# Two blocks instead of one pass mixing and routing first, in plain fp32, and the second of them is gathered for one expert table and dense for the other

## The chip, the cores and the metric

The kernel runs on one core of a Trainium2 chip. The metric is device time in microseconds of one execution: 1673.88 us is the median of three runs of the kernel before (1673.73 to 1687.47). TensorE does the matrix products, VectorE (DVE) and ScalarE (ACT) the elementwise work, GpSimd (POOL) issues the gathers of table rows, and SyncE (SP) issues nearly all other transfers.

## The reference, cut to what matters

512 tokens of width 1024 are worked in four blocks of 128. One layer is mixing, then a product-key expert lookup (PEER), then a last norm:

```
xn = rmsnorm(h);  z = xn @ w_in + b_in              # 1024 -> 3840, split into q k v pool gates
y_a = sliding_window_attention(q, k, v) @ w_attn_up # window 128: own block and the one before
y_p = multiscale_pool(pz) @ w_pool_up
h   = h + (sigmoid(ga) * y_a + sigmoid(gp) * y_p) @ w_o
xn  = rmsnorm(h);  q = xn @ w_query                 # 8 heads, two halves of 128
sc  = q . sub_keys -> top 16 per half -> 256 sums -> top 16 = idx, softmax = g
a   = gelu(u_tab[idx] . xn)                         # 128 experts for each token, of 16384
h   = h + sum(g * a * v_tab[idx]);  out = rmsnorm(h)
```

The two expert tables have 16384 rows of 1024 floats, 64 MB each. For a token block the lookup can be done in two ways. It can be **gathered**: 128 times, one row per token is fetched (128 rows, 512 KB) and multiplied on DVE. Or it can be **dense**: the whole table is streamed through TensorE for all tokens of the block, and the gate matrix (zero for the experts not chosen) picks the results.

## The kernel before, in words

Weights come as tiles of 128x1024 (512 KB). A matrix product is made in one of two ways. Plain fp32 uses the tile as it lands. The three-term form (`mm3`, L114) splits both operands into a high and a low part of the faster fp32r kind and adds hi*hi, hi*lo and lo*hi; each streamed tile then costs a cast on ACT (`wh`, L127) and a subtraction on DVE (`wl`, L121).

The program has these stages. `lead` (L203) takes block 0 alone through mixing and key scores in plain fp32, 128 columns wide. `mixing`, `residual` and `scores` (L334, L580, L622) take blocks 1 to 3 through the same steps in the three-term form, 384 columns wide; beside it `tick` lets background work go on, which is the choice of block 0's experts (`select`) and its gathers (`gather`, L898: 128 rows of the first table, dotted on DVE at L906, and 128 of the second, added at L910). Then 128 expert tiles of the first table are streamed (`u_part`, L781): 24 matmuls of 384 columns each give all three blocks' products. Beside it, blocks 2 and 3 are chosen, and their gate matrices are built and written out (`onehot`, L729: for each 8 tokens eight Abs and eight Relu instructions on ACT, one comparison on DVE, eight plain matmuls, one copy on ACT). Block 1's products are stored (`late`), since its own 128 are later picked from them by element gathers.

In the last stage (`dense`, L856) 128 tiles of the second table are streamed for blocks 2 and 3: 12 matmuls of 512 columns per tile, the left sides made from the kept products (`ga`) and the gates (`gt`) by `mix`. Beside it `gather_late` (L877) fetches 128 rows of the second table for block 1 and adds them on DVE (L895). `final` writes the blocks.

The order of work is written out by hand: `Background` runs a generator until a credit is spent, and `R_A`, `T_Z`, `T_A` and the like are the credits per step. In the last stage each engine's program order is the written order. Rows fetched by POOL wait in a ring of `ROWS` buffers, streamed tiles in a ring of `RAW`.

Of the kernel before, what the change touches and what calls it, by code (L numbers as in the profile page):

```python
# [11 lines left out]
F32 = mybir.dt.float32  # L12
# [7 lines left out]
P = 128  # L20
# [8 lines left out]
PH = 8  # L29
# [11 lines left out]
LB = 1  # L41
VB = 2
NV = 2
TU = SEQ - P
NT = TU // P
# [3 lines left out]
AJ = 4  # L49
# [12 lines left out]


class Layer:
    def __init__(self, ctx, tc, a):
# [6 lines left out]
        self.work, self.owed = [], 0.0  # L72
# [9 lines left out]
        self.natg = c.tile([P, D], F32, name="natg")  # L82
        self.svg = c.tile([P, 16, TOPK], F32, name="svg")
        self.sig = c.tile([P, 16, TOPK], U32, name="sig")
        self.eig = c.tile([P, P], I32, name="eig")
        self.gwg = c.tile([P, P], F32, name="gwg")
        self.hspill = nc.dram_tensor("hspill", (NBLK - 1, P, D), F32, kind="Internal").ap()
        self.ahead = nc.dram_tensor("ahead", (NKEY, P, TD), F32, kind="Internal").ap()
        self.late = nc.dram_tensor("late", (NKEY * P * P, 1), F32, kind="Internal").ap()
        self.spill = nc.dram_tensor("spill", (NG, P, NKEY, TG), F32, kind="Internal").ap()  # L90

    def consts(self):
# [6 lines left out]
        self.tok = self.c.tile([P, 1], I32, name="tok")  # L99
        self.nc.sync.dma_start(out=self.tok, in_=a["tok"])  # L100
# [22 lines left out]
    def weights(self, src, late=False):  # L123
        raw, hi, lo = (self.w.tile([P, D], t, name="w" + n, tag="w" + n, bufs=b)
                       for n, t, b in (("r", F32, RAW), ("h", F32R, WB), ("l", F32R, WB)))
        self.nc.sync.dma_start(out=raw, in_=src)
# [6 lines left out]
    def plan(self, keys):  # L133
        self.keys, self.ready = list(keys), []

    def fetch(self, name, i, look=LOOK):
        while self.keys and len(self.ready) <= look:
            n, j = self.keys.pop(0)
            self.ready.append(((n, j), self.weights(self.a[n][j])))
        key, w = self.ready.pop(0)  # L140
        assert key == (name, i)
        return w
# [11 lines left out]
    def transpose_split(self, x, n, hi, lo):  # L154
        nc = self.nc
        ps = self.big([P, n, P], "tr")
        for k in range(n):
            nc.tensor.transpose(ps[:, k, :], x[:, k * P:(k + 1) * P], self.ident)
        self.split(ps, hi, lo)

    def pair(self, pool, tag, nt=TU):
        return tuple(pool.tile([P, KD, nt], F32R, name=tag + n, tag=tag + n, bufs=1) for n in "hl")
# [18 lines left out]
    def z_block(self, f, xn, dst):  # L181
        w = self.fetch("w_in", f)
        ps = self.mm_tile(TU)
        for k in range(KD):
            if k == KD // 2:
                yield 1
            c = slice(k * P, (k + 1) * P)
            self.mm3(ps, (w[0][:, c], w[1][:, c]), (xn[0][:, k, :], xn[1][:, k, :]), k == 0, k == KD - 1)
        self.nc.scalar.activation(dst, ps, AF.Identity, bias=self.b_in[:, f:f + 1])

    def zq(self, mp, qs, xn, f):
        if f % 2 == 0:
            qs[f // 2] = mp.tile([P, 2, TU], F32, name="q", tag="q", bufs=3)
        return self.z_block(f, xn, qs[f // 2][:, f % 2, :])

    def tick(self, amount):
        for w in self.work:
            if not w.done:
                with self.tc.issue_after(self.lowered):
                    w.spend(amount)  # L200
                return

    def lead(self, mp, t2, t4, kT, vn, carry, g, prologue, rest, others):  # L203
        nc, a = self.nc, self.a
        one = self.m.tile([P, 3, KD, P], F32, name="mh", tag="mh", bufs=1)
        two = self.m.tile([P, 24, P], F32, name="ml", tag="ml", bufs=1)
        xT, att, mT = one[:, 0], one[:, 1], one[:, 2]
        gates, qa = two[:, :16], two[:, 16:]
        yT = mp.tile([P, 4, P], F32, name="yh", tag="yh", bufs=1)

        def raw(src):
            w = self.rows.tile([P, D], F32, name="row", tag="row")
            nc.sync.dma_start(out=w, in_=src)
            return w
# [12 lines left out]
        def across(src):  # L227
            ps = self.big([P, KD, P], "tr")
            for k in range(KD):
                nc.tensor.transpose(ps[:, k, :], src[:, k * P:(k + 1) * P], self.ident)  # L230
            nc.scalar.copy(xT, ps)

        def attended(c, po):
            nc.scalar.copy(att[:, c, :], po)

        def pooled(j, y):
            nc.vector.tensor_copy(yT[:, j, :], y)
# [40 lines left out]
        while active:  # L278
            step()
# [825 lines left out]
```

## Time and profile before

| what | value |
|---|---|
| median of 3 runs | 1673.88 us |
| the profiled execution | 1678.03 us |
| its span, first to last instruction | 1676.0 us |
| PE, DVE, ACT, POOL busy | 90%, 76%, 50%, 40% |
| granted TensorE clock, mean | 0.961 |
| moved by DMA | 476.41 MB, mean 284 GB/s |

A share of the whole span is a mean over stages that are limited by different things. So the rows below are cut by stage. PE is the matmuls, PEld the weight loads that overlap with them; a plain fp32 matmul appears as two instructions, so x16 is eight of them.

### The profile page before, as it was taken

Reading aid. Unit: us, or ns where it says so; the run is one execution under the profiler, and the core shown is the slowest. Engines: PE = TensorE matmul, PEld = TensorE weight load, DVE = VectorE, ACT = ScalarE, POOL = GpSimd, SP = SyncE. Lnnn points to the kernel's source line nnn. Section 1 sums busy time; section 2 is a strip of 40 time slices with the busy share of each in tenths; the row PEclk is TensorE's granted clock in tenths of the full one; section 3 lists DMA queues with packets and bytes.
Section 4 is the critical chain, followed back from the end, with each engine's and each line's share of the span. In section 5 each row is a group of like instructions: output and inputs, shape, how many; then the busy total and the mean of one; then the engine's idle time right before and its main releaser. Section 6 shows DMA issues by size and latency. Waiting matters only on the chain.

```text
span 1676.0 us, 23878 instructions
## 1 busy us (share of the span) xinstructions
PE 1515.9 (90%) x8234; PEld 1356.9 (81%) x8234; DVE 1276.3 (76%) x2395; ACT 835.7 (50%) x1663; POOL 668.8 (40%) x518
## 2 busy tenths in 40 slices
PE   6898979999779989789999999999789898888887
PEld 5797967899679979789999999999766665666665
DVE  2402878889857999977789876677379898898898
ACT  4411346643234333399994999833334343333344
POOL 0000010255520024544435544354277776676730
PEclk9998989999889999989999999999899999999999
DMA  7685242499973348789999999998689999999995
GB/s 270 229 296 206 70 162 94 161 349 341 363 263 105 129 157 295 258 289 344 334 356 316 381 354 345 360 323 313 188 278 357 357 343 369 358 376 372 347 358 206
DMA packets 189465, 476.41 MB, mean 284 GB/s; under 512 B 21408, under 2 KB 84896, under 8 KB 187040
## 3 DMA queue, kind: packets, MB, share of 16 engines
q1 hardware_dynamic: 128736, 270.31, 45.5%
q0 software_dynamic: 59392, 201.42, 34.1%
q10 hardware_dynamic: 1216, 3.15, 0.6%
q8 instruction: 65, 1.06, 0.3%
q14 instruction: 56, 0.46, 0.1%
HBM read 438.50 MB, written 35.78 MB: 283 GB/s over the span
## 4 chain that ended last, share of the span: by engine, by line
PE 28%; DMA 10%; ACT 9%; DVE 7%; issue 4%; POOL 1%; DVEq 0%; ACTq 0%; POOLq 0%
DMA wr<-v_experts 8%; PE mm L116 6%; PE mm L117 6%; PE mm L118 6%; DVE wl L121 4%; PE acc L117 4%; PE acc L118 3%; PE acc L116 3%; ACT wh L127 2%; ACT ohj L752 2%; ACT ohj L746 2%; PE pg L764 2%; ACT gs L765 1%; POOL act L882 1%; DVE h L895 1%
## 5 line engine op out<-in xcount | busy, mean ns | idle before, releaser
L121 DVE TENSOR_TENSOR wl<-wr,wh 128x1024 fp32r<-128x1024 f32 x315 | 385.5, 1225 | 199.0 <-ACT wh L127 196.7
L116 PE MATMUL mm<-xh,wh 128*128 128x384 f32 (+1 forms) x1408 | 486.3, 346 | 19.1 <-ACT gk L795 16.6
L127 ACT CAST wh<-wr 128x1024 fp32r<-128x1024 f32 x315 | 331.9, 1054 | 331.6 <-PE mm L117 239.0
L118 PE MATMUL mm<-xh,wl 128*128 128x384 f32 (+1 forms) x1408 | 479.7, 341 | 7.3 <-DVE wl L121 7.3
L117 PE MATMUL mm<-xl,wh 128*128 128x384 f32 (+1 forms) x1408 | 479.0, 340 | 5.6 <-DVE xl L121 5.6
L873 POOL DMA_INDIRECT row<-u_experts,eig x128 | 196.8, 1537 | 602.6 <-DVE hg L910 250.7
L116 PEld LDWEIGHTS mm<-xh,wh 128*128 128x128 f32 x1408 | 267.8, 190 | 27.1 <-ACT gk L795 19.4
L118 PEld LDWEIGHTS mm<-xh,wl 128*128 128x128 f32 x1408 | 267.7, 190 | 8.8 <-DVE wl L121 8.8
L117 PEld LDWEIGHTS mm<-xl,wh 128*128 128x128 f32 x1408 | 267.7, 190 | 6.0 <-DVE xl L121 5.8
L117 PE MATMUL acc<-wl,wh 128*128 128x512 f32 x512 | 220.3, 430 | 33.3 <-DVE wl L121 30.8
L873 POOL DMA_INDIRECT row<-v_experts,eig x128 | 174.6, 1364 | 187.0 <-DVE row L906 130.9
L116 PE MATMUL acc<-wh 128*128 128x512 f32 x512 | 210.6, 411 | 27.3 <-ACT wh L127 17.8
L118 PE MATMUL acc<-wh,wl 128*128 128x512 f32 x512 | 208.6, 407 | 0.0
L873 POOL DMA_INDIRECT row<-v_experts,ei x128 | 146.6, 1145 | 101.6 <-DVE h L895 76.0
L882 POOL DMA_INDIRECT act<-late,ea x128 | 150.1, 1173 | 80.2 <-DMA late<-a 41.5
L117 PEld LDWEIGHTS acc<-wl,wh 128*128 128x128 f32 x512 | 101.2, 198 | 95.3 <-DVE wl L121 76.2
L832 ACT CAST wh<-wf 128x256 fp32r<-128x256 f32 x128 | 52.1, 407 | 241.2 <-DVE wf L830 201.1
L906 DVE SCALAR_TENSOR_TENSOR row<-row,natg 128x1024 f32<-128x1024 f32 x128 | 155.8, 1221 | 18.4 <-DMA row<-u_experts,eig 18.3
L895 DVE SCALAR_TENSOR_TENSOR h<-row,act,h 128x1024 f32<-128x1024 f32 x128 | 163.9, 1280 | 4.4 <-DMA row<-v_experts,ei 3.7
L910 DVE SCALAR_TENSOR_TENSOR hg<-row,act,hg 128x1024 f32<-128x1024 f32 x128 | 164.1, 1282 | 3.3 <-DMA row<-v_experts,eig 2.7
L116 PEld LDWEIGHTS acc<-wh 128*128 128x128 f32 x512 | 100.9, 197 | 58.5 <-ACT wh L127 26.1
L118 PEld LDWEIGHTS acc<-wh,wl 128*128 128x128 f32 x512 | 101.1, 198 | 18.6
(245 smaller groups left out, 1850.9 us busy)
## 6 DMA issues: line engine op xcount, KB each, us to landing
wr<-u_blocks SPq DMA_DIRECT2D x128, 512.0 KB, 5.8
wr<-v_experts SPq DMA_DIRECT2D x128, 512.0 KB, 6.5
spill<-gs SPq DMA_DIRECT2D x16, 1024.0 KB, 8.9
gt<-spill SPq DMA_DIRECT2D x64, 256.0 KB, 8.1
row<-w_in SPq DMA_DIRECT2D x30, 512.0 KB, 4.3
wr<-w_in SPq DMA_DIRECT2D x30, 512.0 KB, 3.8
row<-w_query SPq DMA_DIRECT2D x16, 512.0 KB, 4.3
wr<-w_query SPq DMA_DIRECT2D x16, 512.0 KB, 3.4
```

The lines of the kernel that those rows point to most:

```text
L116: mm(out, lhsT=l[0], rhs=r[0], start=first, stop=False)
L117: mm(out, lhsT=l[0], rhs=r[1], start=False, stop=False)
L118: mm(out, lhsT=l[1], rhs=r[0], start=False, stop=last)
L121: self.lowered = self.nc.vector.tensor_tensor(lo, src, hi.bitcast(F32), op=ALU.subtract).ins
L127: self.nc.scalar.copy(hi, raw)
L746: nc.scalar.activation(ohj[:, z, :], self.iota, AF.Abs, bias=tr[:, 1, u + z:u + z + 1])
L832: nc.scalar.copy(wh, wf)
L873: self.nc.gpsimd.indirect_dma_start(out=t, out_offset=None, in_=tab, in_offset=bass.IndirectOffsetOnAxis(ap=ei[:, s:s + 1], axis=0))
L882: nc.gpsimd.indirect_dma_start(out=act[:, s:s + 1], out_offset=None, in_=self.late, in_offset=bass.IndirectOffsetOnAxis(ap=ea[:, s:s + 1], ...
L895: nc.vector.scalar_tensor_tensor(z, v, act[:, s:s + 1], z, op0=ALU.mult, op1=ALU.add)
L906: nc.vector.scalar_tensor_tensor(u, u, 1.0, xn, op0=ALU.mult, op1=ALU.mult, accum_out=act[:, s:s + 1])
L910: nc.vector.scalar_tensor_tensor(z, v, act[:, s:s + 1], z, op0=ALU.mult, op1=ALU.add)
```

## The change

Blocks 0 and 1 now go first, and 2 and 3 after them. Both pairs pass the same `mixing` generator, 256 columns wide, with every product in plain fp32: the two `mm3` splits of the streamed tiles in mixing, residual and scores are gone (59 of the 315 casts and as many subtractions, and those of attention, pooling, merge and `w_o`), and `lead`, `residual` and `scores` with them. The norms, transposes and the key and value projections of the second pair are begun at the end of the first.

Block 1 is chosen beside the second pair's mixing. Its 128 rows of the first table are gathered (`dots`), its gate matrix is built from the finished products g*a with signs (`spread(CB)`, all on DVE by a fused compare and multiply), and for the second table it is dense, as blocks 2 and 3 are. So the first table is dense for 256 columns (24 matmuls of 256 per tile), the second for three blocks (18 matmuls of 512 per tile), and the store of block 1's products, the element gathers and the tile of token numbers go. Of the 384 row gathers, 128 move from the second table to the first. For blocks 2 and 3 five of eight one-hot rows are built on ACT, three on DVE. Block 0 is finished at the end and no longer before the last stage.

```diff
-LB = 1
+CB = 1
 VB = 2
-NV = 2
-TU = SEQ - P
+HALF = 2
+TU = HALF * P
+NV = 3
-R_A = 3.8
-LAG = 8
-T_Z, T_A, T_O, T_W, T_S = 7.0, 0.5, 2.0, 1.2, 0.0
+R_A = 3.4
+R_U = 0.9
+T_Z, T_A, T_O, T_W, T_S = 7.0, 2.0, 2.6, 2.5, 0.9
-U_S = 4
-LOOK = 2
+LAG = 4
-HELD = (42, 50)
+HELD = (46, 23)
+ZA = 5
-RAW, ROWS, WB = 3, 5, 3
+RAW, ROWS, WB = 4, 6, 3
...
         def z(f, dst, w=None):
-            if w is None:
-                w = raw(a["w_in"][f])
-            ps = self.mm_tile(P)
-            mm(ps, w, xT)
-            self.copied = nc.scalar.activation(dst, ps, AF.Identity, bias=self.b_in[:, f:f + 1])
+            ps = self.mm_tile(TU)
+            mm(ps, w or self.raw(a["w_in"][f]), xT)
+            self.paced = nc.scalar.activation(dst, ps, AF.Identity, bias=self.b_in[:, f:f + 1])
...
+            two = self.mixing(mp, HALF, xn2, (nothing, nothing, nothing))
+            one = self.mixing(mp, 0, None, (rest, self.consts, lambda: next(two)))
+            for _ in one:
+                pass
...
+            self.near = Background(picked(CB))
+            self.dotted = [Background(self.dots(CB, 0, 40)), Background(self.dots(CB, 40, P))]
+            self.work = [self.near, self.dotted[0], Background(picked(GB)), self.dotted[1],
+                         Background(self.gather())]
+            for _ in two:
+                pass
...
         def build(n, ohj):
             u = 8 * n
-            for z in range(8):
+            for z in range(za, 8):
+                v.tensor_scalar(ohj[:, z, :], self.iota, tr[:, 4, u + z:u + z + 1], tr[:, 2, u + z:u + z + 1],
+                                op0=ALU.is_equal, op1=ALU.mult)
+            for z in range(za):
...
     def u_part(self, n, w, xn2):
         nc = self.nc
-        ps = self.project(w, xn2, slice(0, TU))
-        if n % AJ == 0:
-            self.a1 = self.ga.tile([P, AJ, P], F32, name="a1", bufs=2)
-        nc.scalar.activation(self.a1[:, n % AJ, :], ps[:, :P], AF.Gelu)
...
+        for k in range(KD):
+            c = slice(k * P, (k + 1) * P)
+            self.mm3(ps, (w[0][:, c], w[1][:, c]), (xn2[0][:, k, :], xn2[1][:, k, :]), k == 0, k == KD - 1)
...
         yield
+        nc.scalar.copy(h1, g1)
         nc.vector.tensor_tensor(wf.rearrange("p (g t) -> p g t", t=TG), ga.rearrange("p (g t) -> p g t", t=TG),
-                                gts[m // NI][:, :, m % NI, :], op=ALU.mult)
-        nc.scalar.copy(wh, wf)
+                                g[:, N1:], op=ALU.mult)
+        nc.scalar.copy(wh[:, P:], wf)
         self.ws[m] = (wh, wl)
         yield
-        self.low(wf, wh, wl)
+        self.low(g1, h1, l1)
+        self.low(wf, wh[:, P:], wl[:, P:])
...
-    def dense(self, acc, fetch):
-        rate = PH * TOPK / (NKEY - 3 - LAG)
+    def dense(self, acc):
+        rate = self.units / (NKEY - 2 - LAG)
...
-            bg = Background(choose(2), choose(3), spread(2), choose(LB), spread(3))
-            rate = (2 * PH * TOPK - fetch.spent) / (NKEY - ahead - 4)
+            bg = Background(choose(2), choose(3), spread(2), spread(3), spread(CB))
```

**The order in the last stage.** On DVE, the end of one tile and the next whole tile, with the last 16 weights of block 1 made ready (`act`) between. `wl<-wr,wh` is the low part of the table tile, `wf` the left side, `h` the sum for block 1. Before:

```order
L121 TENSOR_TENSOR wl<-wr,wh 128x1024
L830 TENSOR_TENSOR wf<-gar,gt 128x256
L890 TENSOR_TENSOR act_11136<-act_11136,gw_3869 128x16
L895 SCALAR_TENSOR_TENSOR h_11121<-row,act_11136,h_11121 128x1024
L121 TENSOR_TENSOR wl<-wf,wh 128x256
```

One added row stands in each tile. In the changed kernel, one tile and the head of the next:

```order
L657 TENSOR_TENSOR wf<-gar,gt 128x256
L707 SCALAR_TENSOR_TENSOR row,act_98<-row,nat_80 128x1024
L730 SCALAR_TENSOR_TENSOR hg<-row,act_98,hg 128x1024
L119 TENSOR_TENSOR wl<-gt,wh 128x128
L119 TENSOR_TENSOR wl<-wf,wh 128x256
L119 TENSOR_TENSOR wl<-wr,wh 128x1024
```

What moved: most tiles carry two units, a dot (L707) and an add (L730) for block 0, some carry one, and a low part of the gates of block 1 is new. Counted over DVE's whole order, 70 of the 384 units stand ahead of the first expert tile, 114 in the stage of the first table and 200 in the last stage, where there were 128.

**The order around the second pair's residual.** On DVE, from the choice of block 0 to the norm of block 2 (`t_2913` is block 2's sum, `nat_81` the normed block 1 that the dots use):

```order
L531 CAST ei_90<-sk 128x128
L534 RECIPROCAL sk<-sk 128x8
L707 SCALAR_TENSOR_TENSOR row,act_99<-row,nat_81 128x1024
L535 TENSOR_TENSOR gw_94<-gw_94,sk 128x128
L707 SCALAR_TENSOR_TENSOR row,act_99<-row,nat_81 128x1024 x14
L307 TENSOR_TENSOR t_2913<-ho,t_2913 128x1024
L707 SCALAR_TENSOR_TENSOR row,act_99<-row,nat_81 128x1024 x3
L142 RECIPROCAL r<-sd 128x1
L143 SCALAR_TENSOR_TENSOR t_2917<-t_2913,r,gf 128x1024
```

Before, at the residual of blocks 1 and 2 (`hb` is the sum, `natg` the normed block 0, `hg` its sum):

```order
L906 SCALAR_TENSOR_TENSOR row,act<-row,natg 128x1024
L608 TENSOR_TENSOR hb<-ho,hb 128x1024 x2
L910 SCALAR_TENSOR_TENSOR hg<-row,act,hg 128x1024
L906 SCALAR_TENSOR_TENSOR row,act<-row,natg 128x1024
L151 RECIPROCAL r<-sd 128x1
L910 SCALAR_TENSOR_TENSOR hg<-row,act,hg 128x1024
L152 SCALAR_TENSOR_TENSOR nat<-hb,r,gf 128x1024
```

What moved: single rows of the background stood between the steps of the residual; now fifteen dots stand in one run ahead of block 2's sum, and three more between the sum and its norm.

## Rows read from the trace of the kernel before

**Rows 1.** Busy time by stage: stretch, its length, busy us, clock, DMA share, GB/s.

```profile
0.00:178.00 178.00, 148.17 (x1104) 134.07 (x1104) 51.69 (x187) 54.77 (x130) 0.69 (x6) 0.94 0.70 240
178.00:592.00 414.00, 374.70 (x2153) 345.69 (x2153) 341.85 (x857) 179.47 (x334) 107.12 (x82) 0.96 0.58 208
592.00:720.00 128.00, 114.06 (x618) 111.46 (x616) 127.12 (x357) 47.18 (x95) 56.41 (x31) 0.96 0.70 238
592.00:1200.00 608.00, 586.45 (x3445) 582.51 (x3443) 479.80 (x817) 418.63 (x927) 264.31 (x174) 0.98 0.87 309
910.00:1080.00 170.00, 168.64 (x1050) 168.07 (x1049) 126.44 (x144) 162.32 (x373) 78.98 (x56) 1.00 0.98 358
1209.00:1664.00 455.00, 403.30 (x1525) 292.62 (x1525) 396.49 (x523) 179.16 (x261) 292.73 (x252) 0.95 0.97 344
1230.00:1650.00 420.00, 370.82 (x1403) 268.50 (x1401) 372.00 (x484) 162.18 (x234) 276.00 (x238) 0.95 1.00 357
```

**Rows 2.** Timeline of PE, plain fp32 in `lead`: start, us, instruction, count.

```profile
120.27 13.90 PE L302 MATMUL ho<-row,mh 128*128 128x512 f32 x32
...
149.78 1.95 PE L218 MATMUL mm<-mh,row 128*128 128x128 f32 x16
151.56 0.39 PE L315 MATMUL mm<-sk,t 128*128 128x128 f32 x2
```

**Rows 3.** Timeline of PE, three-term form at 256 and at 512 columns.

```profile
484.44 0.28 PE L116 MATMUL mm<-xh,wh 128*128 128x256 f32 x1
...
486.84 0.28 PE L118 MATMUL mm<-xh,wl 128*128 128x256 f32 x1
...
1460.26 0.40 PE L117 MATMUL acc<-wl,wh 128*128 128x512 f32 x1
...
1465.51 0.39 PE L116 MATMUL acc<-wh 128*128 128x512 f32 x1
```

**Rows 4.** Timeline of PE, the last piece of an attention unit.

```profile
253.90 1.09 PE L547 MATMUL mm<-t,vn 128*64 128x256 f32 x8
```

**Rows 5.** Waits of PE from 0 to 592 us: total, times, longest.

```profile
PE pt L540 <- DVE t L534: 12.5, 5, 8.5
```

**Rows 6.** DVE by line, 592 to 722 us: count, busy us, mean ns, idle before.

```profile
L121 DVE TENSOR_TENSOR wl<-wr,wh 128x1024 fp32r<-128x1024 f32 x26 | 31.9, 1228 | 0.9 <-ACT wh L127 0.8
L906 DVE SCALAR_TENSOR_TENSOR row<-row,natg 128x1024 f32<-128x1024 f32 x17 | 20.8, 1223 | 0.0
L910 DVE SCALAR_TENSOR_TENSOR hg<-row,act,hg 128x1024 f32<-128x1024 f32 x16 | 20.5, 1284 | 0.0
```

**Rows 7.** Timeline of ACT while gate matrices are built.

```profile
943.04 2.04 ACT L765 COPY gs<-pg 128x1024 f32<-128x1024 f32 x1
944.84 2.46 ACT L746 ACTIVATE ohj<-iota,tr 128x128 f32<-128x128 f32 x8
947.18 0.89 ACT L752 ACTIVATE ohj<-ohj,tr 128x128 f32<-128x128 f32 x2
947.95 1.06 ACT L127 CAST wh<-wr 128x1024 fp32r<-128x1024 f32 x1
948.89 0.29 ACT L786 ACTIVATE a<-mm 128x128 f32<-128x128 f32 x1
949.05 0.39 ACT L795 ACTIVATE ga<-mm 128x256 f32<-128x256 f32 x1
```

**Rows 8.** Timeline of DVE, one tile of the last stage.

```profile
1399.90 1.28 DVE L895 SCALAR_TENSOR_TENSOR h<-row,act,h 128x1024 f32<-128x1024 f32 x1
1401.10 0.42 DVE L121 TENSOR_TENSOR wl<-wf,wh 128x256 fp32r<-128x256 f32 x1
1401.49 1.23 DVE L121 TENSOR_TENSOR wl<-wr,wh 128x1024 fp32r<-128x1024 f32 x1
1402.63 0.42 DVE L830 TENSOR_TENSOR wf<-gar,gt 128x256 f32<-128x256 f32 x1
1402.97 1.28 DVE L895 SCALAR_TENSOR_TENSOR h<-row,act,h 128x1024 f32<-128x1024 f32 x1
```

More of the change, by code (lines that the diff above doesn't have):

```diff
@@ L131, in weights, with raw @@
         return (hi, lo), lambda: self.low(raw, hi, lo)
[L133 to L141, printed above, removed]
+    def raw(self, src):
+        w = self.w.tile([P, D], F32, name="wr", tag="wr", bufs=RAW)
+        self.nc.sync.dma_start(out=w, in_=src)
         return w
@@ L179, in project, with feed, tick, mixing @@
         return ps
[L181 to L196, printed above, removed]
+    def feed(self, amount):
         for w in self.work:
             if not w.done:
-                with self.tc.issue_after(self.lowered):
-                    w.spend(amount)
+                w.spend(amount)
                 return
-    def lead(self, mp, t2, t4, kT, vn, carry, g, prologue, rest, others):
+    def tick(self, amount):
+        with self.tc.issue_after(self.paced.ins):
+            self.feed(amount)
+    def mixing(self, mp, b0, xn2, hooks):
         nc, a = self.nc, self.a
[L205 to L214, printed above, removed]
+        bs = range(b0, b0 + HALF)
+        first = b0 == 0
+        rows = [slice(j * P, (j + 1) * P) for j in range(HALF)]
+        xT = self.m.tile([P, KD, TU], F32, name="xT", tag="xT", bufs=2)
+        def t2():
+            return mp.tile([P, TU + 16], F32, name="t2", tag="t2", bufs=7)
+        def t4():
+            return mp.tile([P, D], F32, name="t4", tag="t4", bufs=4)
+        def tick(amount):
+            if not first:
+                self.tick(amount)
         def mm(ps, w, x, nk=KD):
@@ new lines, in mixing @@
+        for x, b in zip(xs, bs):
+            nc.sync.dma_start(out=x, in_=a["x"][0, b * P:(b + 1) * P, :])
+            if b == GB:
+                self.gm = mp.tile([P, D], F32, name="gm")
+                nc.scalar.dma_start(out=self.gm, in_=a["ln_mix_g"][0].partition_broadcast(P))
+        w89 = [None, None]
+        if first:
+            w89 = [self.raw(a["w_in"][f]) for f in (8, 9)]
+            hooks[0]()
+        for x, r in zip(xs, rows):
+            n = t4()
+            self.norm(x, self.gm, n)
+            self.across(n, lambda ps, r=r: nc.scalar.copy(xT[:, :, r], ps))
@@ new lines, in mixing @@
+            tick(2.5 * T_O)
+        if first:
+            self.gf = mp.tile([P, D], F32, name="gf")
+            nc.scalar.dma_start(out=self.gf, in_=a["ln_ffn_g"][0].partition_broadcast(P))
+        ps = [self.big([P, 2, 512], "ho") for _ in bs]
+        for k in range(KD):
+            w = self.raw(a["w_o"][k])
+            for j, r in enumerate(rows):
+                for n in range(2):
+                    nc.tensor.matmul(ps[j][:, n, :], lhsT=mT[:, k, r], rhs=w[:, n * 512:(n + 1) * 512],
+                                     start=k == 0, stop=k == KD - 1)
+            tick(T_W)
@@ L997, in run @@
-            with tc.tile_pool(name="score", bufs=1, side="right", reuse_waits="tile") as sp:
-                subk = sp.tile([P, 16, P], F32, name="subk")
-                nc.scalar.dma_start(out=subk, in_=a["sub_keys"])
-                for i, _ in enumerate(self.scores(xn2, sp, sv, si, subk)):
-                    if i % U_S == U_S - 1:
-                        part()
-                    self.tick(T_S)
+                if b == CB:
+                    while not self.dotted[1].done:
+                        self.feed(1)
+                    jf[b] = self.indices(tp, self.ei[b])
@@ L1010, in run @@
                     bg.spend(R_A)
-                    fetch.spend(rate)
+                    self.feed(R_U)
+            print("one-hot done at", ahead, "units left", self.units)
         self.home, self.room = self.pool("more", 1, reuse_waits="tile"), HELD[1]
```

599 lines of the change are left out of this document (197 added, 402 removed).

## The prediction

> **What bounds the kernel now.** I cut the span into stages first, since its busy shares are means over unlike stages [rows 1]. The pass of block 0 takes 178 us, the mixing, residual and scores of blocks 1 to 3 take 414, the first table 608, and 9 us later the last stage takes 455; 12 us are left for the end. In the first table's stage TensorE is the bound: it is busy 586 of 608 us, and in the densest stretch 99%, beside ACT at 95% and DMA at 98%. The last stage is not bound by it: between 1230 and 1650 us TensorE is busy 88%, at a clock of 0.95, while DMA is at 1.00 and moves 357 GB/s. One tile there takes 3.07 us when nothing is late, and that is DVE without a gap [rows 8]; 128 of them would be 393, and the rest of the 455 is waiting for transfers. Then I read what one instruction costs from start to start in the timelines, because neighbours overlap and busy durations are too long.
>
> **Prices on TensorE.** Plain fp32: eight matmuls of 128 columns in 1.78 us, 0.223 each, and sixteen of 512 in 13.90, 0.869 each [rows 2]. A line through both gives 0.438 for 256 columns. Three-term: twenty matmuls of 256 in 2.40 us, 0.120 each; 23 of 512 in 5.25, 0.228 each [rows 3]. So a tile of the first table needs 24 x 0.120 = 2.88 us, a tile of the second 18 x 0.228 = 4.11 (12 x 0.228 = 2.74 before).
>
> **First pair.** 464 products (30 projections, 8 tiles of w_attn_up, 4 of w_pool_up, 16 of w_query) x 0.438 = 203; w_o 32 x 0.869 = 28; key scores 32 x 0.223 = 7. An attention unit has three pieces on TensorE of eight instructions each; one takes 1.09 us [rows 4]. With the others put at as much, a unit is about 3.2, half that for block 0, which sees one key block: 19. Pooling and transposes 6. Sum 263. Block 0 alone needed 133 by the same prices and took 178, so 45 went to the start, the chain of attention through DVE and ACT, and the clock. Most of it stays; the residual's part, some 10, is now covered by the second pair's first projections (16 products, 7 us; without them the 10 come back), and each product lasts twice as long over the same chain. I take 32: **295**.
>
> **Second pair.** 267 by the same sum. Here DVE, in program order, has half of block 1's choice ahead of the first attention unit, and ten dots ahead of the last two; TensorE waits for the transposes of each. The longest such wait before was 8.5 us [rows 5]; a whole choice is 26 (of the 127 us that DVE was busy from 592 to 720 [rows 1], some 73 are the work of [rows 6], and the rest holds two choices). Between 8 and 40 in all, I take 25: more than one wait, less than both in full. At the residual fifteen dots stand ahead of block 2's sum. They lie beside the 28 us of w_o, but the three dots, one dot and two dots that follow stand inside the sum and norm of both blocks, at 1.22 each with 1.2 for each of five other steps: 14 to 20 us in which TensorE has nothing, I take 18. With 3 for the clock: **313**. The two pairs end at 608. Before, the same work ended at 592 with four tiles of the first table inside (17 us), so the splits' removal gives nothing back: a plain product at 0.438 costs more than three terms at 0.120, and that eats what TensorE lost to waiting for the splits.
>
> **First table.** By DVE's order the stage has four parts. (a) 31 tiles beside the choice of blocks 2 and 3: DVE needs 31 x 1.14 (the subtraction, start to start [rows 8]) + 52 + 18 dots x 1.22 = 109, TensorE 89: 113. (b) 55 tiles beside two gate matrices. On ACT [rows 7] an Abs is 0.293, a Relu 0.385, the copy 1.80, the cast 0.94, the gelu about 0.3; a group of eight tokens now costs 5 x 0.678 + 1.80 = 5.19 (7.2 before), so ACT needs 55 x 1.24 + 32 x 5.19 = 234, TensorE 55 x 2.88 + 256 x 0.223 = 215, DMA (55 tiles, 56 gathered rows, 16 MB of gates, 40 stored tiles, 80 MB) 224 at 357 GB/s: 240. (c) 24 tiles beside block 1's gate matrix, whose one-hot rows are on DVE: TensorE 69 + 28 = 97, DVE about 88: 100. (d) 18 tiles alone: 54. Together **507**, plus 4 to open; TensorE's own share of it is 454. Before it was 608.
>
> **Last stage.** 200 of the 384 units are left for it. DVE per tile: 1.14 + 0.39 + 0.34, a low part of 128 columns that no row shows (between 0.2 and the 0.39 of 256 columns, 0.26 taken, since it is half as wide), and 200/128 x 1.21 = 1.89, sum 4.02. TensorE: 4.11. DMA: 67 MB of tiles, 105 MB of rows, 25 MB of gates (three blocks for two), 8 MB of reloaded products: 205 MB, where the stretch of 1.00 moved 150 in 420 us [rows 1]. At its 357 GB/s that is 575 us, 4.5 per tile. So transfers end last, as they do now, and TensorE has a tenth of slack where it had a fifth; a late tile also lowers its clock (0.95 in that stretch). I take **585**, between 526 (TensorE alone) and 615 (both losses added). Before: 455. The element gathers and the 8 MB of stores for them go; they lay beside other work and were under 2% of the bytes, so I count nothing. POOL's 238 issues took 276 us there, 1.16 each [rows 1]; 200 are 232 us of 585, no bound.
>
> **Sum.** 608 + 4 + 507 + 9 + 585 + 15 for the end (four blocks to write instead of three) = 1728, against a span of 1676.0, whose execution took 1678.0: 1730 us. The median is 0.25% under that execution; I forecast **1728 us, slower by 3%**. Within 1% is 1657 to 1691, about what a measurement of this kernel can tell from no change. That the instructions are as described is read from the order of the changed program, so I give no chance to a change that does not do what it says.
>
> **Rivals.**
> 1. TensorE paces every stage, so the kernel is faster. Its sums are 263 + 267 + 454 + 526 = 1510. In the first table's stage before, its sum was 124 x 24 x 0.174 (384 columns, on the line through the two three-term prices) + 256 x 0.223 = 575 of 608, 94.6%, beside nearly full ACT and DMA. If that ratio holds everywhere: 1596 + 9 + 13 + 15 + 2 = 1635. It decides where DVE's and DMA's loads stay under TensorE's in a stage; against it stand part (a), the last stage's 575 and the long runs of dots. Chance 0.13.
> 2. Only the last stage is at TensorE's pace: the 357 GB/s were no ceiling but what that stage asked for, and 205 MB flow in 540. Then 1728 - 45 = 1683, no change. For it: some slices of the page reach 381. Against it: DMA at 1.00 for 420 us while ACT waits for tiles. Chance 0.2.
> The Trainium skill, DMA: Bandwidth & Descriptors, section Bandwidth, gives 425 GB/s for a 16 MB load by one core whose neighbour is idle; by it the 205 MB would take 483 us and TensorE would set the stage. The trace does not agree: its longest full stretch moved 357.
> 3. Worse: at each late tile the stage loses transfers' time and TensorE's low clock (4.8 per tile, 615), and the second pair waits 40 us longer for DVE: 1728 + 30 + 40 = 1798. Chance 0.12.
>
> **Chances and range.** The forecast has 0.55, its own range 1695 to 1765. Faster by over 1%: 0.13; within 1%: 0.19, nearly all of rival 2; slower: 0.68. For 8 in 10 the range has to take in rival 2 and half of rival 3: 1665 to 1790.
>
> **What would show it.** In the changed profile the first table should start near 608 us, with TensorE waiting on DVE once early in the second pair and for 14 us or more before its w_query products. The first table should take about 510 us, with ACT over 90% busy while two gate matrices are built. The last stage should show DMA at 1.00 and some 357 GB/s, TensorE near 92%, about 4.55 us per tile. I am wrong if the last stage takes 545 or less, if its DMA moves over 375 GB/s, or if both pairs are done before 575 us.

## The result: slower by 4.85%, and the profile after

The changed kernel takes 1763.29 us (median of 4 runs, 1754.47 to 1765.70), the kernel before on the same chip 1679.79 (4 runs): a ratio of 1.0485, with a 95% interval of 1.0417 to 1.0553. The forecast was 1728, so the sign and the range held and the size did not. The profiled execution took 1754.47 us with a span of 1752.7; the sum of the forecast was made against a span and gave 1728, so 25 us have to be found. That execution is the shortest of the four; against the median it would be some 9 us more.

The same table by stage as [rows 1], of the changed kernel: stretch, its length, busy us of PE, PEld, DVE, ACT and POOL, clock, DMA share, GB/s. The borders are the end of the first pair's scores (300), the first expert tile (639), the first and the last gate row built on ACT (764, 987), the last gate product (1100), the last product of the first table (1166), and the first and last matmul of the last stage.

```profile
0.00:300.00 300.00, 277.89 (x1309) 225.44 (x1310) 83.94 (x321) 74.20 (x180) 0.69 (x6) 0.99 0.43 146
300.00:639.00 339.00, 274.70 (x1242) 220.10 (x1240) 224.37 (x730) 71.08 (x167) 96.09 (x76) 0.90 0.63 228
639.00:764.00 125.00, 103.33 (x797) 99.03 (x797) 124.41 (x373) 53.30 (x77) 31.94 (x21) 0.95 0.66 227
764.00:987.00 223.00, 199.27 (x1596) 193.21 (x1597) 176.39 (x284) 217.75 (x443) 65.07 (x50) 0.97 0.91 316
987.00:1100.00 113.00, 112.99 (x958) 111.88 (x958) 112.77 (x217) 71.26 (x77) 35.14 (x24) 1.00 0.97 351
1100.00:1166.00 66.00, 61.86 (x500) 59.80 (x499) 45.16 (x49) 27.75 (x42) 24.33 (x20) 1.00 0.95 351
1173.00:1743.00 570.00, 541.44 (x2302) 436.06 (x2303) 501.75 (x814) 207.49 (x398) 282.03 (x194) 0.98 0.97 351
1200.00:1700.00 500.00, 472.03 (x2007) 379.18 (x2006) 444.24 (x724) 179.38 (x342) 266.38 (x183) 0.98 1.02 369
1743.00:1752.70 9.70, 0.81 (x4) 0.35 (x2) 6.67 (x16) 3.53 (x13) 0.00 (x0) 0.74 0.44 162
```

Read each row for the engine that has no gap. In the first pair it is PE (278 of 300, and DVE, ACT and DMA are all under half). In the second pair it is none: PE has 275 of 339 at a mean clock of 0.90 (1.0 is 2.4 GHz, so for part of the time it had the lower level, 1.2), so it waits. In the four parts of the first table it is DVE (124.4 of 125), ACT (218 of 223), PE and DVE together (113) and PE (62 of 66). In the last stage PE is busy 95% and DMA at 0.97 to 1.02; a table of busy shares can't tell which of the two ends last, and that was the first question for experiments.

| stage | forecast | measured |
|---|---|---|
| first pair | 295 | 300 |
| second pair | 313 | 339 |
| first table, with its opening and the 4 us | 520 | 534 |
| last stage | 585 | 570 |
| end | 15 | 10 |

Against the kernel before, the mixing of all blocks lost 64 us (639 against 575, when the four tiles inside its 592 are taken off), and the two tables lost 15 (1104 from the first expert tile to the last matmul, against 608 + 17 + 9 + 455 = 1089). So most of the loss lies in the part from which work was taken out.

### The profile page after: what moved, and what is told of

The parts are those of the page before. It is cut to its first block, busy times and chain, and to the rows that moved or that the text cites. A ratio compares the mean times of both kernels' runs of the same rounds, so it can differ in the third digit from the quotient of the medians.

```text
span 1752.7 us, 24708 instructions
## 1 busy us (share of the span) xinstructions
PE 1572.9 (90%) x8701; PEld 1346.2 (77%) x8701; DVE 1275.5 (73%) x2797; ACT 726.9 (41%) x1391; POOL 535.3 (31%) x390
## 4 chain that ended last, share of the span: by engine, by line
PE 31%; ACT 10%; DMA 8%; DVE 6%; issue 3%; SPq 0%; DVEq 0%; ACTq 0%
DMA wr<-v_experts 7%; PE acc L115 6%; PE acc L116 6%; PE acc L114 6%; PE mm L114 4%; PE mm L116 3%; PE mm L115 3%; DVE wl L119 3%; ACT wh L124 3%; ACT gs L589 2%; PE pg L588 2%; ACT ohj L576 2%; ACT ohj L567 2%; DVE row L707 1%; DMA gar<-ahead 1%
## 5 line engine op out<-in xcount | busy, mean ns | idle before, releaser
L701 POOL DMA_INDIRECT row<-u_experts,ei x256 | 342.6, 1338 | 944.4 <-DVE row L707 406.0
L198 PE MATMUL mm<-xT,wr 128*128 128x256 f32 x1472 | 337.1, 387 | 3.3 <-ACT xT L312 2.2
L114 PE MATMUL mm<-xh,wh 128*128 128x256 f32 x1024 | 296.2, 291 | 28.6 <-ACT gk L618 12.7
L707 DVE SCALAR_TENSOR_TENSOR row<-row,nat 128x1024 f32<-128x1024 f32 x256 | 309.6, 1217 | 15.4 <-DMA row<-u_experts,ei 15.0
L198 PEld LDWEIGHTS mm<-xT,wr 128*128 128x128 f32 x1472 | 282.1, 194 | 45.9 <-issue 3.4
L114 PE MATMUL acc<-wh 128*128 128x512 f32 x768 | 303.5, 395 | 14.7 <-ACT wh L124 7.7
L116 PE MATMUL acc<-wh,wl 128*128 128x512 f32 x768 | 302.5, 394 | 0.0
L116 PE MATMUL mm<-xh,wl 128*128 128x256 f32 x1024 | 288.4, 285 | 15.6 <-DVE wl L119 15.0
L115 PE MATMUL mm<-xl,wh 128*128 128x256 f32 x1024 | 288.7, 283 | 0.0
L114 PEld LDWEIGHTS mm<-xh,wh 128*128 128x128 f32 x1024 | 193.8, 190 | 37.0 <-ACT gk L618 16.1
L114 PEld LDWEIGHTS acc<-wh 128*128 128x128 f32 x768 | 146.3, 191 | 50.2 <-ACT wh L124 11.4
L730 DVE SCALAR_TENSOR_TENSOR hg<-row,act,hg 128x1024 f32<-128x1024 f32 x128 | 163.6, 1278 | 0.5
L588 PE MATMUL pg<-ohi,ohj 128*128 128x128 f32 x768 | 103.0, 285 | 7.0 <-ACT ohj L576 6.6
```

Source lines behind the costliest of these rows:

```text
L114: mm(out, lhsT=l[0], rhs=r[0], start=first, stop=False)
L115: mm(out, lhsT=l[0], rhs=r[1], start=False, stop=False)
L116: mm(out, lhsT=l[1], rhs=r[0], start=False, stop=last)
L198: nc.tensor.matmul(ps, lhsT=w[:, k * P:(k + 1) * P], rhs=x[:, k, :], start=k == 0, stop=k == nk - 1)
L588: nc.tensor.matmul(pg[:, z, :], lhsT=ohj[:, z, :], rhs=ohi[:, z, :], start=True, stop=True)
L701: self.nc.gpsimd.indirect_dma_start(out=t, out_offset=None, in_=tab, in_offset=bass.IndirectOffsetOnAxis(ap=ei[:, s:s + 1], axis=0))
```

## The experiments

Each is an edit of the changed kernel. Stage times are from one profiled execution each; where a whole time is compared, its number of runs is given. Stages whose code is the same show how far single executions agree. In the changed kernel and the five runs that leave both pairs and the first table's stage alone or nearly so, the first pair ended at 296 to 300 us, the second pair took 337 to 341, and the first table 526 to 528. The last stage repeats less well: with the same 200 rows and the same work it took 570 us in the changed kernel, and 582, 582 and 586 in three runs below that change only the mixing. Two of them, the three-term and the timed one-pass run:

```profile
1172.00:1754.00 582.00, 548.90 (x2304) 441.35 (x2304) 503.38 (x815) 208.42 (x400) 283.22 (x194) 0.97 0.96 344
```

```profile
1035.00:1621.00 586.00, 549.70 (x2304) 441.54 (x2304) 503.25 (x815) 208.07 (x400) 282.11 (x194) 0.97 0.95 342
```

So a difference of 10 or 15 us in the last stage, between two single executions, shows little by itself. The runs without row fetches, with short sums, with two blocks and without background were made on another chip than the rest; the kernel before took 1692.43 us there and 1681.49 to 1685.52 on the chip of the others.

### What ends last in the last stage

**Without its row fetches.**

```diff
-                if m >= LAG:
-                    self.feed(rate)
```

> Left out: the 200 row fetches of block 0 that fall into the last stage, and their arithmetic (block 0's sum stays incomplete). Everything before that stage is unchanged. The last stage took 570 us in the changed kernel, with TensorE busy 541 of them. Theory (transfers end last, at 369 GB/s): without 105 of its 205 MB the stage has 100 MB, 270 us, and TensorE sets it: 526 to 545 us. Rival (TensorE paces the stage already, and its losses are its own: clock, chain from the table tile through ACT and DVE): 560 to 570 us, no change worth naming.

The stage of that run: PE has no gap in it, and DMA is at little more than half.

```profile
1168.00:1693.00 525.00, 524.54 (x2303) 434.12 (x2304) 292.38 (x515) 199.81 (x388) 0.00 (x0) 0.99 0.58 188
```

525 us: the theory's number, and the 526 of the forecast's TensorE sum. So TensorE did not set the 570, although it was busy 95% of them; 45 us or more were due to the rows. They bring transfers and DVE work, which the next runs separate.

**The rows stay, most of their arithmetic goes.**

```diff
-        self.nc.vector.scalar_tensor_tensor(u, u, 1.0, self.nat[b], ...
+        w = slice(0, self.cut)        # 128 of 1024 columns
+        self.nc.vector.scalar_tensor_tensor(u[:, w], u[:, w], 1.0, self.nat[b][:, w], ...
```

> Left out: seven eighths of the arithmetic on the 200 rows fetched in the last stage (128 of 1024 columns are multiplied and added). All row fetches stay, so the bytes are the same, and DVE is relieved of about 1.1 us for each of 200 rows, 220 of its 502 us there. Theory (transfers end last): the stage stays within 10 us of 570. Rival (DVE's queue makes the low parts of the table tiles late): it falls to 545 or less. Second rival (TensorE paces): also within 10 us of 570; the run with twelve matmuls per tile tells the two apart.

**Block 1's matmuls go, everything else stays.**

```diff
         for c in range(NV):
+            if c == 0 and 0 < n < NKEY - 1:
+                continue
```

> Left out: block 1's six matmuls in the inner 126 of the 128 tiles of the last stage (its sum stays incomplete). Transfers, ACT and DVE do what they did. TensorE needs 128 x 2.74 = 351 us there in place of 526. Theory (transfers end last, 205 MB at 369 GB/s = 556 us): the stage stays at 545 to 570 us. Rival (TensorE paces): it falls to what DVE needs, 4.02 per tile, 515 us, or near it (500 to 530).

**Both at once.**

> Left out in the last stage: block 1's matmuls in the inner 126 tiles, and seven eighths of the arithmetic on the fetched rows. So TensorE has 351 us of work there and DVE about 290; all 205 MB are still moved. Theory (transfers alone set the stage at 357 to 376 GB/s): 545 to 573 us, as with either part left out by itself. Rival (TensorE and DVE each hold it when the other is light): 530 or less.

The stage in these three, in this order:

```profile
1171.00:1729.00 558.00, 537.82 (x2301) 437.52 (x2302) 340.21 (x814) 206.03 (x398) 199.61 (x194) 0.98 0.99 359
```

```profile
1168.00:1741.00 573.00, 427.05 (x1545) 306.92 (x1546) 499.76 (x814) 214.44 (x398) 302.75 (x194) 0.92 0.97 349
```

```profile
1172.00:1729.00 557.00, 425.40 (x1546) 304.96 (x1547) 328.75 (x815) 214.19 (x399) 219.84 (x194) 0.89 0.99 359
```

A third of TensorE's matmuls can go and the stage takes 573 instead of 570. Seven eighths of DVE's row arithmetic can go and it takes 558, which is 12 less (two more than the theory allowed). With both gone it takes 557, 16 less than with the arithmetic left in. What all three still have in common is 200 MB of transfers at 349 to 359 GB/s with DMA at 0.97 to 0.99. So transfers hold the stage, DVE's load adds 12 to 16 (two pairs of runs that agree; one alone would show little), and block 1's six matmuls per tile cost nothing there as long as TensorE's whole sum stays under what the transfers need. How early a transfer can start is set by the two rings of buffers, whose sizes no run varied; that deeper rings would not raise the rate is argued from the DMA share near 1. The waits of ACT for table tiles move as they should: 39.4 us in the changed kernel and 97.1 in the last of these runs, where everything else is light (ACT is also what casts the tile for TensorE):

```profile
ACT wh L656 <- PE acc L115: 236.6, 99, 4.8
...
ACT wh L124 <- DMA wr<-v_experts: 39.4, 21, 4.4
```

```profile
ACT wh L124 <- DMA wr<-v_experts: 97.1, 28, 11.2
```

The first of these rows shows how a list of waits misleads. In the changed kernel ACT waits six times longer for PE than for DMA, since it runs ahead and is held by the buffer that PE still reads. That is what a wait on the engine ahead of it looks like in a stage that this engine does not set.

### What the second pair pays

**No background beside it.** Experts fixed, no choice and no dot before the first table.

```diff
-            self.near = Background(picked(CB))
+            for b in (CB, GB):
+                nc.vector.tensor_copy(self.ei[b], self.iota)
...
+            self.work = []
```

> Left out: the choice of experts of blocks 0 and 1 (they get fixed numbers 0 to 127), and all background work beside the second pair; the dots follow in the later stages, whose times are therefore not compared. The second pair's mixing, residual and scores took 336 us (303 to 639), the first pair 296 with 10 us of loading at its start. Theory (DVE's background rows ahead of attention, pooling and residual make TensorE wait, about 55 us in all): 275 to 290 us, so the pairs end near 585. Rival (the chain of attention through DVE and ACT, and the clock, cost it as much without any background): 315 us or more.

The second pair took 291.8 us (298.96 to 590.72) in place of 340: 48 are the background's (45 to 49 against the 337 to 341 above). The theory's number (275 to 290) was too low by 2 to 17, so part of the rival holds. Its window and what PE still waits for:

```profile
299.00:590.00 291.00, 267.44 (x1243) 215.97 (x1241) 94.83 (x364) 68.18 (x164) 0.00 (x0) 0.96 0.37 129
```

```profile
PE pt L440 <- DVE t L434: 11.3, 8, 4.6
PE tr L148 <- DVE t L143: 9.6, 2, 5.6
```

These 21 us are the chain of attention and that of the residual, with no background on DVE (busy 95 of 291 us). In the changed kernel the same waits of PE, from 300 to 639 us (they answer to [rows 5]), are:

```profile
PE tr L148 <- DVE t L143: 21.4, 2, 13.1
PE pt L439 <- DVE den L431: 20.0, 1, 20.0
PE mm L474 <- DVE t L468: 7.9, 2, 4.8
PE pt L439 <- DVE den L432: 5.1, 1, 5.1
```

The 20.0 is a single wait: the sum of the first attention unit (`den`) stands on DVE behind a run of the choice. This is DVE's timeline there; `sk`, `gw` and the comparisons with `iota` and `fewpos` are the choice, `t`, `mx` and `den` the attention:

```profile
319.60 1.55 DVE L526 TENSOR_TENSOR t<-fewpos,sk 128x640 f32<-128x640 f32 x2
321.07 1.55 DVE L528 TENSOR_TENSOR t<-t,sk 128x640 f32<-128x640 f32 x2
322.54 1.53 DVE L529 TENSOR_REDUCE sk<-t 128x32 f32<-128x640 f32 x2
324.00 2.34 DVE L418 SCALAR_TENSOR_TENSOR t<-s,mask 128x1024 f32<-128x1024 f32 x2
326.26 2.33 DVE L422 TENSOR_REDUCE mx<-t 128x4 f32<-128x1024 f32 x2
...
332.54 0.15 DVE L431 TENSOR_TENSOR den<-den,sk 128x4 f32<-128x4 f32 x1
332.62 0.27 DVE L533 TENSOR_REDUCE sk<-gw 128x8 f32<-128x128 f32 x1
```

**No rows from `w_o` on.** `T_O` 2.8, `T_W` and `T_S` 0; 36 of 70 rows move later.

```diff
-T_Z, T_A, T_O, T_W, T_S = 7.0, 2.0, 2.6, 2.5, 0.9
+T_Z, T_A, T_O, T_W, T_S = 7.0, 2.0, 2.8, 0.0, 0.0
```

> Nothing is left out. The second pair's w_o, residual and scores run without background rows; the credits ahead of them are a little larger, so that both choices still end in time. 36 of the 70 rows that were fetched and dotted beside that pair go to the last stage. Theory (rows of block 1 stand between the steps of the residual on DVE and cost the pair some 20 us of its 48): the first expert tile starts near 618 us instead of 639, and the last stage, with 236 rows instead of 200, takes 570 + 36 x 0.524 MB / 0.369 = 620 us, so the kernel is slower than the changed one, near 1785. Rival (the stall at the residual is the chain of sum, norm and transposes itself): the first expert tile at 632 or later, total 1800.

The first expert tile started at 626.6, between the two: the pair took 329, so the residual's part is some 11 us. The wait of 20.0 is unchanged and that of `tr` falls from 21.4 to 9.3. Where the rows went I had wrong. Only ten reach the last stage (588 us for 210 rows); the other 26 are dotted in the first table, since block 1's gates need all its dots, and there DVE is the bound in part: 571 us in place of 534, 1.4 us for each row.

```profile
PE pt L439 <- DVE den L431: 20.0, 1, 20.0
PE tr L148 <- DVE t L143: 9.3, 2, 5.3
```

```profile
627.00:1198.00 571.00, 489.86 (x3848) 474.05 (x3847) 481.70 (x956) 368.62 (x633) 179.29 (x134) 0.95 0.86 305
1198.00:1786.00 588.00, 550.48 (x2301) 438.22 (x2302) 513.25 (x830) 209.23 (x399) 303.32 (x204) 0.97 0.97 349
```

The kernel took 1797.54 us (one run).

**The same work in even small credits.**

```diff
-T_Z, T_A, T_O, T_W, T_S = 7.0, 2.0, 2.6, 2.5, 0.9
+T_Z, T_A, T_O, T_W, T_S = 2.5, 3.0, 3.2, 0.0, 0.9
```

> Nothing is left out. The same two choices and most of the rows beside the second pair, dealt out in even small credits: 2.5 in place of 7.0 at its start, 3.0 and 3.2 later, none in w_o. Ten rows move to the last stage (210 in place of 200). Theory (the first attention unit stands behind one long piece of the choice on DVE, 20 us, and rows stand between the steps of the residual, some 13 us): the first expert tile starts 25 to 33 us earlier, near 610, the last stage takes 10 x 1.4 = 14 us more, and the kernel falls by 10 to 20 us. Rival (DVE has the same work in the same stretch, so the waiting only moves to other attention units and to pooling): the first expert tile at 630 or later, the kernel unchanged or 10 us slower.

The first expert tile started at 610.1, the second pair took 315, and the kernel 1748.96 us (4 runs, 1747.20 to 1750.75): 1.0384 of the kernel before, interval 1.0346 to 1.0421, where the changed kernel has 1.0485 (1.0417 to 1.0553): about 1% less. The two intervals just meet, so the size of this gain is not clear of noise, although all four runs lie below all four of the changed kernel. The theory held for the pair. PE's longest waits there are now:

```profile
PE tr L148 <- DVE t L143: 12.1, 2, 8.1
PE pt L439 <- DVE den L431: 10.3, 1, 10.3
```

In the profiled execution most of what the pairs won, 29 us, is lost again, because the last stage takes 592 us for ten more rows: 22 more than the 570 and 6 to 10 more than the 582 to 586 of the other runs, where 14 was expected.

### The end of the first table

**No rows after the last gate product.**

```diff
-            with tc.issue_after(part()):
-                self.feed(R_U)
+            part()
```

> Nothing is left out. After the last gate matrix, the remaining tiles of the first table run without row fetches; their 19 rows go to the last stage (219 in place of 200). That stretch took 72 us (1100 to 1172) with DMA at 0.95 and TensorE busy 62. Theory (transfers set it): it falls to TensorE's pace, 58 to 62 us, and the last stage grows by 19 x 0.524 MB / 0.369 = 27 us to 597; the kernel is slower by some 15 us. Rival (the chain ACT, DVE, TensorE of each tile sets it): 68 us or more.

That stretch took 65 us in place of 66 (69 in place of the 72 named above, which runs on to the opening of the last stage), with DMA at 0.57 in place of 0.95: the rival. The whole first table took 526.7 us, in the changed kernel 526.9. A DMA share of 0.95 had set nothing there; that each tile waits for TensorE (busy 60 of 65 us) and the chain behind it is how I read it. The last stage took 602 for 219 rows, 32 more than the 570 and 16 to 20 more than the 582 to 586, where 27 was expected, and the kernel took 1781.97 (one run).

```profile
1100.00:1165.00 65.00, 59.75 (x481) 57.49 (x479) 23.29 (x19) 26.03 (x40) 0.00 (x0) 1.00 0.57 200
1169.00:1771.00 602.00, 557.41 (x2304) 440.28 (x2304) 524.65 (x845) 210.16 (x401) 322.39 (x213) 0.97 0.97 349
```

### What plain fp32 costs in mixing

**The first pair's projections in the three-term form again.**

```diff
+            if lo is not None:
+                h, l = (mp.tile([P, D], F32R, ...) for n in "hl")
+                self.split(w, h, l)
+                for k in range(nk): self.mm3(ps, (h[:, c], l[:, c]), (x[:, k, :], lo[:, k, :]), ...)
```

> Nothing is left out. The first pair's 30 projections (240 of its 464 products) go back to the three-term form, with a cast on ACT and a subtraction on DVE for each tile; the rest of both pairs stays plain. On TensorE 240 x (0.438 - 3 x 0.120) = 19 us less. Theory (TensorE paces the first pair, it was busy 281 of 303 us there; ACT and DVE have 75 and 86 us of work): the first pair falls by 15 to 20 us from 300, and the kernel by as much, to about 1745. Rival (the extra casts and subtractions lengthen the chain of each projection by as much as TensorE saves): the first pair at 295 to 305, the kernel at 1755 to 1765.

The rival: the first pair ended at 298.1 and the kernel took 1763.22 us (4 runs, 1757.85 to 1777.94; 1.0487 of before, 1.0412 to 1.0563). The trace shows where. Most of the 16 gate projections follow each other without a gap, and each ends in a copy on ACT; these copies are 3.45 us apart in the changed kernel and mostly 2.85 here, as the prices say. ACT, gate projections, first of the changed kernel, then of this one:

```profile
115.99 0.47 ACT L203 ACTIVATE gates<-mm,b_in 128x256 f32<-128x256 f32 x1 [0.61 <-PE mm L198]
119.44 0.47 ACT L203 ACTIVATE gates<-mm,b_in 128x256 f32<-128x256 f32 x1 [2.98 <-PE mm L198]
```

```profile
133.20 0.47 ACT L212 ACTIVATE gates<-mm,b_in 128x256 f32<-128x256 f32 x1
136.04 0.47 ACT L212 ACTIVATE gates<-mm,b_in 128x256 f32<-128x256 f32 x1
```

That is 9 us for sixteen. But from the first copy of a query to the first copy of pooling it took 51.3 us here (31.28 to 82.61) against 49.6 in the changed kernel (30.24 to 79.84). In between stand the eight attention units; that their chain through DVE and ACT does not shorten when TensorE needs less, and that the splits join it, is argued. A gap of 6 us among the first gates took back most of the 9. The edit also makes room by taking one of the seven `t2` buffers away, which pooling uses, and no run separates this from the splits.

**One pass.** The operands are rounded to the fast kind by ACT and multiplied once.

```diff
+        def one(w):
+            o = mp.tile([P, D], F32R, name="wx", tag="wx", bufs=2)
+            nc.scalar.copy(o, w)
+            return o
...
-        xT = self.m.tile([P, KD, TU], F32, name="xT", tag="xT", bufs=2)
+        xT = self.m.tile([P, KD, TU], F32R, name="xT", tag="xT", bufs=2)
```

> Left out: the accuracy of 464 products in each pair (projections, w_attn_up, w_pool_up, w_query), which are made in one pass from operands rounded to the fast kind; each streamed tile is cast on ACT first (about 1.05 us each). At 0.120 us for 256 columns in place of 0.438, TensorE has 148 us less in each pair. Theory (the first pair is paced by TensorE with some 30 us of its own chain): 296 falls to 150 to 185. Rival (most of the pair is the chain through DVE and ACT and the loading of 58 tiles at 512 KB, so the plain products are hidden): 230 or more. In the second pair, with DVE's background unchanged at about 225 us busy, both theories expect less gain: 240 to 270 from 341.

> The same program as the run with one-pass products, timed: 1628 us within 0.5%, against about 1680 of the kernel before, a ratio of 0.97. Theory and rival expect the same here; the run gives the interval.

The first pair took 208 us and the second 284, up to the first expert tile at 492.4 (490.3 in the timed run): between theory and rival for the first, above both for the second. The whole took 1627.66 us (4 runs, 1620.96 to 1631.92), 0.9654 of the kernel before (0.9612 to 0.9696), and 136 under the changed one. The pairs of the timed run:

```profile
0.00:207.00 207.00, 149.61 (x827) 112.85 (x828) 72.62 (x244) 131.01 (x242) 0.69 (x6) 0.88 0.61 212
207.00:490.00 283.00, 151.16 (x795) 113.25 (x793) 226.02 (x764) 122.49 (x222) 95.00 (x74) 0.76 0.73 269
```

TensorE lost 128 us of busy time in the first pair and the pair 93; in the second it lost 124 and the pair 56, because DVE's work, 226 us of 283, is all still there, and PE waited 57.0 us for it in attention (waits of PE from 208 to 521 us, in the first of the two runs):

```profile
PE pt L447 <- DVE den L439: 57.0, 3, 38.3
PE tr L148 <- DVE t L143: 23.0, 2, 15.7
```

**One pass with the even credits.**

> One-pass products (the 464 of each pair rounded to the fast kind, as before) together with the evenly dealt background. In the run with one-pass products the second pair took 312 us, with TensorE waiting 57 us for DVE in its attention and 23 at its residual, and DVE busy 255. Theory (the order of DVE's work makes the waits): 275 to 290 us, the last stage 14 us longer, the kernel 10 to 20 us below the one-pass kernel, near 1612. Rival (DVE's load itself holds the pair): 300 us or more, the kernel at 1625 to 1645.

For the whole time, the rival: 1628.46 us (4 runs; 0.9692 of before, 0.9632 to 0.9751), no better than without. For the pair, neither. The 312 above was read up to 520 us, which is 28 us after the first expert tile had begun; up to that tile the pair took 284 in the run before and 276 here (204.3 to 480.1). So the even credits won some 8 us, where 22 to 37 were expected, and the last stage took 593 us for 210 rows against 582 and 586 for 200. The longest wait shrank from 38.3 to 28.7, and DVE's waits for rows grew to 29.6 from 17.9 and 20.9 in the two runs before, part of them in a stretch in which DMA is full.

```profile
204.00:480.00 276.00, 158.92 (x799) 120.77 (x798) 211.08 (x728) 123.52 (x224) 71.94 (x61) 0.73 0.68 252
320.00:380.00 60.00, 40.38 (x186) 34.90 (x184) 41.02 (x130) 35.59 (x44) 29.19 (x27) 0.64 1.03 409
```

```profile
PE pt L447 <- DVE den L439: 36.1, 2, 28.7
...
DVE row L715 <- DMA row<-u_experts,ei: 29.6, 24, 3.9
```

So the version that beats both kernels is the one with one-pass mixing. It is not the same arithmetic: its projections carry fewer bits, and what the same rounding would give the kernel before was not tried. With the arithmetic kept, nothing tried here came under the kernel before; the best was 1748.96.

## Why the prediction was right in sign and short by 25 us of span

**What bounds which stage** was right at all the places that decide it. The first pair ended at 300 where 295 was forecast. Two gate matrices went at ACT's pace: for the 46 tiles that fell into that stretch the forecast's own formula, 46 x 1.24 + 32 x 5.19, gives 223, and it took 223. The last stage was held by transfers, and TensorE's sum of 526 came out as 525 when the rows were taken away.

**The step that failed is the second pair: "267 by the same sum", to which 43 us of background and 3 for the clock were added and nothing else.** The first pair had been given 32 for its start, its chain of attention and the clock; the second got 3 of these, for the clock alone. The run without background measures both parts: 48 for the background, where 25 + 18 was forecast, and 292 for the pair itself, where 270 was. Sixteen of its 464 products lie in the first pair's residual, so its sum in that stretch is 260, and its own loss is 32, as much as the first pair had been given. (The sum itself is some 3 short: all eight attention units of this pair see two key blocks, 25.6 us in place of 19, which makes 270; the loss is then 29.) Of the loss, 21 are the two waits shown above; for the rest, PE was busy 267 us at a clock of 0.96, and there are small gaps. Within the background the parts were off the other way round: the residual's was some 11 where 18 was taken, so 37 lie ahead of it where 25 was.

The pair's 26 us are as much as the whole error of 25 in the profiled execution, since the other stages' errors, +5, +14, -15 and -5, cancel. That is luck, and partly that of the execution: its last stage is the shortest seen with these rows and this work. Of the other three executions no trace is kept; their 7 to 11 us more may lie there.

**The first table** was short by 14. Its parts held 33, 46, 28 and 21 tiles where 31, 55, 24 and 18 were read from the order (eight instructions of L114 to a tile, counted in the same four stretches):

```profile
639.00:764.00 125.00, 76.77 (x265) 51.20 (x265) 0.95 0.66 227
764.00:987.00 223.00, 107.31 (x367) 69.08 (x367) 0.97 0.91 316
987.00:1100.00 113.00, 65.41 (x226) 42.52 (x226) 1.00 0.97 351
1100.00:1166.00 66.00, 46.40 (x166) 30.89 (x167) 1.00 0.95 351
```

By the forecast's prices these counts give 115, 223, 109 and 60. The parts are 10, 0, 4 and 6 over. In the first DVE is busy without a gap, and the counts were short: its rows hold 35 subtractions and 22 dots where the sum for 33 tiles has 33 and 18, some 7 us. The rest, the two choices and the search of the last key scores, is 58 us by the same prices (124.4 - 35 x 1.14 - 22 x 1.22) where 52 was taken. It was 57 already in [rows 1] and [rows 6] (127 - 26 x 1.14 - 33 x 1.22); the forecast had subtracted busy durations there, which overlap. From the first part, DVE:

```profile
L119 DVE TENSOR_TENSOR wl<-wr,wh 128x1024 fp32r<-128x1024 f32 x35 | 42.0, 1212 | 0.6 <-issue 0.3 <-ACT wh L124 0.3
L707 DVE SCALAR_TENSOR_TENSOR row<-row,nat 128x1024 f32<-128x1024 f32 x22 | 26.5, 1207 | 0.0
```

**The last stage** was forecast 15 too long for the profiled execution, and met by the 582 to 586 of the other runs. It moved 200 MB and not 205, at a mean of 351 GB/s, so 570; the 10 us that the forecast laid on top, for late tiles that lower the clock, cannot be seen in it (clock 0.98, where [rows 1] had 0.95). The run with 12 matmuls to a tile, beside the same transfers, shows 0.92. The end took 10 and not 15.

**The rivals.** TensorE does not pace every stage (the quiet pair, the first part of the first table and the last stage each have another limit). That only the last stage goes at TensorE's pace, 540 us, is refuted by the runs in which TensorE or DVE or both are light: the transfers alone need 557. Yet its mechanism was half right, since 357 GB/s is not a ceiling: the stage moved 369 between 1200 and 1700 us, and 409 was seen over 60 us in the one-pass run with even credits. The Trainium skill, DMA: Bandwidth & Descriptors, section Where 436 GB/s comes from, names about 358 GB/s as what the memory gives one core and about 435 as the limit of the fabric: the means over the whole last stage agree with the first figure (342 to 359 in all runs that kept the rows), the stretch at 409 does not, and no run here came to the 425 of its Bandwidth table (the section Bandwidth). The third rival's second half came in part: the second pair took 26 us longer than forecast, but mostly by its own chain (22) and little by DVE's queue (5).

**Where the expected gain went.** Taking out 59 casts and subtractions freed ACT and DVE. That neither of them set mixing is shown for the first pair alone, where putting 30 of each back left its time as it was. TensorE paid for it: a plain product takes 3.45 us for eight where three terms take 2.85. But that is not the whole price, since undoing it for the projections gained nothing. The pair is a chain of attention as well as a queue of products, and two blocks ahead of everything keep the gathers waiting: DMA stands at 0.43 for 300 us, and a row that is put off to the last stage costs something between 1 and 2 us there: 19 rows took 16 to 32 us, and ten rows took 18 and 22 against the 570, but only 2 to 10 against the 582 to 586. At 351 GB/s its 0.524 MB alone are 1.5 us. That an earlier first choice would have won these is argued, and was not tried.

## What to carry to other kernels

A pass that is run twice has its own losses twice: give the second instance what the first one lost in the trace, and add the new waits to it. A stage at a DMA share near 1 may hold an engine that is 95% busy, and only taking that engine's work away tells which of them ends last; here a third of the matmuls was free and a fetched row cost 1 to 2 us. Such a stage is also the one that repeats worst: the same transfers took 570 to 586 us, where each other stage came again within 4, so a small edit is not judged there by one execution. Background work for a shared engine goes in small even pieces ahead of a chain, for one long piece is a wait of its own length.

## What was not expected of the hardware

- The rate at a full DMA share is not one number: 369 GB/s at 1.02 in the last stage, 409 at 1.03 in a stretch of weight tiles and rows (the one-pass run with even credits), 357 at 1.00 in [rows 1].
- The rate of the whole last stage differed between executions with the same 200 rows: 351, 344, 344 and 342 GB/s.
- With a third of its matmuls gone, TensorE's instructions in the last stage were longer: 1545 in 427 us (0.276 each), against 2302 in 541 (0.235), at a mean clock of 0.92 against 0.98.
